# Five small edits in a two-block transformer kernel: dispatch order, slot weights, value width, two queue orders

## The chip, the cores and the metric

The kernel runs on one core of a Trainium2 chip and is written in Bass with the Tile framework, which sets the semaphores between the engines from the tiles that instructions read and write. The metric is the device time of one execution in microseconds, given as the median of several executions.

## What is computed

All data is fp32: 256 tokens of 1024 features. A first block mixes the tokens by a pooling branch and by a differential attention of 8 heads, merges the two by gates, and ends with a feed-forward layer of 4096 hidden features. A second block has latent attention and neighbourhood attention over the tokens and a context of 256 more, and then a mixture of experts in 4 groups of 4. Each token takes one group and two experts of it. Cut to what the change touches:

```python
# first block
h = rmsnorm(x, g_mix)
z = h @ w_in                       # pool 512 | queries 1024 | keys 1024 | values 1024 columns
v = z[..., 2560:3584]
# second block: hx, hc are the normalised, modulated tokens and context
proj = hx @ w_in_2                 # q_lat 384 | na_q 512 | kv_lat 256 | kr 32 | na_k 512 | na_v 512
nk_c, nv_c = (hc @ w_in_2)[..., 672:1184], (hc @ w_in_2)[..., 1184:]
# mixture of experts: g_sel is each token's group, combine its two expert weights
hid = silu(t @ w_gate[e]) * (t @ w_up[e])
y = sum over e of (hid * combine[:, e]) @ w_down[e]
```

The inputs are drawn from a fixed seed, so each group's number of tokens is the same in every execution.

## The kernel before, in words

**Products in three parts.** Up to the experts every fp32 factor is cut into an upper part, rounded to the type `fp32r`, and a lower part, the rest. A product is then three matmuls: upper by upper, upper by lower, lower by upper (`mm3`, or written out in `dense_steps`). Weights come by DMA as blocks of 128 x 2048 into one of four raw buffers. All these loads are issued by SP in the order of the program. `split` (lines 188 to 194) cuts a piece of 1024 columns: ScalarE copies the upper part (line 192) and VectorE subtracts it to get the lower part (line 193). A block takes two such calls.

**Order of the work.** A planner, `J`, runs several generators beside one another. Each yields the TensorE time of what it has just issued (`MM` stands for the three matmuls of 256 columns) or a waiting time or a condition; the planner takes the next step from the lane with the best rank that is ready by its own clock. The result is a fixed order of instructions for each engine; at run time each engine works through its own in order. `order(later, earlier)` sets such an order by hand.

**First block.** The lane `feed` (lines 710 to 729) issues two blocks of the pooling input (`upool`), then for each of four pairs of heads the query block, the key block and the value block `v_block(p)` (lines 540 to 554), then eight gate blocks. Beside it run `stats` (lines 490 and on) and two lanes of attention heads. `stats` computes the squares of x, their means by TensorE (`ms`), the sum `mse` on VectorE (line 498), and from it the root and its reciprocal `rcol`. `v_block` multiplies 8 pieces of the tokens by 256 columns of weights, for each half of the tokens, into one bank of PSUM; the halves share the bank. `scaled_split` then writes the upper part on ScalarE and the lower on VectorE. `mmbank` gives the banks for query, key, value and gate blocks in turn.

**Second block.** `na_values` (lines 954 to 971) does the same for the values of the neighbourhood attention, first for the context, then for the tokens, in two blocks of 256 columns each. `na_pair` (lines 981 to 1004) makes queries and keys for two heads. The lower part of the queries, `ql`, is written twice, to two ranges of partitions, by two VectorE steps per head (lines 999 and 1001).

**Routing and experts.** The tokens of a group are gathered into slots by a product with a one-hot matrix (`gather`, name `xg`, line 1658). A group with more than 64 tokens is *wide* and has 128 slots. Six programs for the experts are in the kernel, called ways here: ways 0 to 3 where one group is wide, the group of that number; way 4 where all are; way 5 in two passes. The number is in memory (`way`); each engine loads it into a register (line 1907) and finds its program by nested comparisons (`ways_from`, lines 1909 to 1923). Its `tc.If` at line 1918 is a COMPARE_BRANCH instruction on each engine's sequencer. In each program 16 turns follow, one for each expert, in the order of `TURNS`: groups 0 and 1 by turns, then groups 2 and 3. A turn has 32 gate and up products (`gate_up`, name `gu`, lines 1765 to 1776), the activation `hidden`, a transposition and 16 or more products with `w_down` (name `y`). `product` makes TensorE keep the written order of all of them. `slot_weights` (lines 1737 to 1748) takes the routing weights of each slot by 16 small products (`sv`), which `gate_up(0, slot_weights)` places between its 16th and 17th product. `hidden` multiplies by these weights. The expert weights are 96 blocks of 1 MB, loaded into a ring of 17 buffers, each load being issued by SP as soon as its buffer has been used.

Of the kernel before, what the change touches and what calls it, by code (L numbers as in the profile page):

```python
# [15 lines left out]
OP = mybir.AluOpType  # L16
# [58 lines left out]
IDLE = (13, 7)  # L75

KEPT = 5

HALF = 64

# [41 lines left out]
def tile_two_blocks(ctx, tc, a):  # L122
# [65 lines left out]
    def split(src, n):  # L188
        t = whl.tile([128, 2048], F32R, name="whl", tag="w")
        hi, lo = t[:, 0:n], t[:, 1024:1024 + n]  # L190
        with tc.high_priority(offset=AHEAD_SPLIT):
            nc.scalar.copy(hi, src)  # L192
            nc.vector.tensor_sub(lo, src, hi)  # L193
        return hi, lo

    def split_fine(w):

# [292 lines left out]
    def stats():  # L490

        with low_priority(SQP):
            acc = squares(xT)
        use_table("natural_log_exp_and_others")
        yield 0, LAT_ST
        ms = bank(7, "ms")
        mean_mm(ms, acc)
        nc.vector.tensor_scalar(mse, ms[:, :2], EPS, None, op0=OP.add)
        nc.vector.tensor_scalar(epsq, mse, EPS, None, op0=OP.mult)
        rstd(rcol, mse, 2)  # L500
        yield 0.43, 2.0
        rb_ps = bank(7, "rb_ps")
        rows_of_cols(rb_ps, rcol)
        nc.vector.tensor_copy(rb, rb_ps[:, :T])
        small_inputs()
        yield 0.86, 0.5, when("u")
        for b in range(2):
            nc.vector.tensor_mul(upad[:, 2 * b:2 * b + 2, 16:], ups[b].rearrange("p (m t) -> p m t", m=2),
                                 rb.unsqueeze(1).to_broadcast([128, 2, T]))
        wg = big(11, [128, 2, 512], F32R, "wg")  # L510
        wgh, wgl = wg[:, 0], wg[:, 1]
        copy_split(wgh, wgl, load(a["w_grp"], (128, 512)))
        for g in range(4):
            yield 0, LAT_POOL
            pool_group(g, wgh, wgl)
            yield 0.35
# [22 lines left out]

    def v_block(b):  # L540

        w = split_block(load(a["w_in"][10 + b]))
        ps = mmbank("v")
        for tb in range(2):
            for k in range(8):
                hi, lo = w(k, 256)
                mm3(ps[:, tb * 256:(tb + 1) * 256],
                    (xh[:, k, tb * 128:(tb + 1) * 128], xl[:, k, tb * 128:(tb + 1) * 128]), (hi, lo),
                    k == 0, k == 7)
                yield MM  # L550
        for tb in range(2):
            scaled_split(vh[:, tb, b * 256:(b + 1) * 256], vl[:, tb, b * 256:(b + 1) * 256],
                         ps[:, tb * 256:(tb + 1) * 256], rcol[:, tb:tb + 1])
        done.add(("v", b))

    def gate_block(g):
        half, j = divmod(g, 4)
# [152 lines left out]
    def feed():  # L710
        for b in range(2):
            ups.append(bank(3 + b, "upool"))
            if b == 0:
                yield from dense_steps(ups[b], split_fine(first), xs, groups=[range(i, i + 2) for i in range(0, 8, 2)])
            else:
                yield from dense_steps(ups[b], split_block(load(a["w_in"][b])), xs)
        done.add("u")
        for p in range(4):
            if p >= 2:
                yield 0, 0, lambda: pair[p - 2]["heads"] == 2  # L720
            yield from qk_block(p, 0)
            yield from qk_block(p, 1)
            yield from v_block(p)
            for i in MODQ[p]:
                mod_block(i, MODS.get(i))
        for n, g in enumerate((0, 4, 1, 5, 2, 6, 3, 7)):
            yield from gate_block(g)
            for i in MODG[n]:
                mod_block(i, MODS.get(i))
# [222 lines left out]
    nav = [value_tile(7), value_tile(8)]  # L952

    def na_values():
        wv = [split_block(load(a["w_in2"][4 + b])) for b in range(2)]
        yield
        for n in range(2):
            if n == 1:
                yield "context"
                yield 0, 3.0, when("hx")  # L960
            for b in range(2):
                ps = mmbank("nav")
                for tb in range(2):
                    for k in range(8):
                        mm3(ps[:, tb * 256:(tb + 1) * 256],
                            (srcs[n][0][:, k, tb * 128:(tb + 1) * 128], srcs[n][1][:, k, tb * 128:(tb + 1) * 128]),
                            wv[b](k, 256), k == 0, k == 7)
                        yield MM
                for tb in range(2):
                  with tc.high_priority(offset=NAVP):  # L970
                    value_split(nav[n], tb, slice(4 * b, 4 * b + 4), ps[:, tb * 256:(tb + 1) * 256])

    def proj(ps, w, c0, n, kt=8, width=256, x=None, koff=0):

# [6 lines left out]
    def na_pair(p):  # L981
# [15 lines left out]
        for j in range(2):  # L997
            nc.scalar.activation(qh[j][rows[j]], psq[rows[j]], AF.Copy, scale=0.125)
            nc.vector.scalar_tensor_tensor(ql[j][rows[j]], psq[rows[j]], 0.125, qh[j][rows[j]], op0=OP.mult, op1=OP.subtract)
            nc.scalar.activation(qh[j][rows[1 - j]], psq[rows[j]], AF.Copy, scale=0.125)  # L1000
            nc.vector.scalar_tensor_tensor(ql[j][rows[1 - j]], psq[rows[j]], 0.125, qh[j][rows[j]], op0=OP.mult,
                                           op1=OP.subtract)
        J.add(0, ready(("na", p), 1.2))
        pair["na", p] = qh, ql, keys, nb

# [667 lines left out]
    def experts(part, wide):  # L1673
# [193 lines left out]
                with tc.high_priority(offset=CHAIN):  # L1867
                    sums[g] = finish(g)

        gate_up(0, slot_weights)  # L1870
        if TURNS[0][0] in wide or TURNS[1][0] in wide:
            rows_of_slots()
        for n in range(16):
# [7 lines left out]
            else:  # L1881
                if n > 0:
                    list(down(n - 1))
                early = n == 0 and not {TURNS[0][0], TURNS[1][0]} & set(wide)
                if early:
                    gate_up(1)
                turn(n)
# [21 lines left out]
    def ways_from(lo, hi):  # L1909

        if hi - lo == 1:
            table["load"], table["uses"] = None, []
            experts(0, (lo,) if lo < 4 else tuple(range(4)))
            if lo == 5:
                experts(1, tuple(range(4)))
            return
        mid = (lo + hi) // 2 if hi <= 4 else max(lo + 1, 4)
        with tc.If(n_way < mid) as cmp:
            ways_from(lo, mid)
        with cmp.Else():  # L1920
            ways_from(mid, hi)
# [26 lines left out]
def layout(i):  # L1948
# [9 lines left out]
    o["cols"] = np.ascontiguousarray(np.concatenate([cols_of(p) for p in parts], axis=1))  # L1958
    o["lambda_qk"] = i["lambda_qk"].reshape(1, 256)
    o["w_in"] = blocks(i["w_in"][0], 256)  # L1960
    o["w_gate"] = blocks(i["w_gate"][0], 256)
    o["w_grp"] = np.ascontiguousarray(i["w_pool_grp"][0].transpose(1, 0, 2).reshape(128, 512))
    o["w_bp"] = blocks(i["w_branch_pool"][0], 512)
# [20 lines left out]
    o["b_mod"] = np.ascontiguousarray(i["b_mod_2"][0].reshape(6, D))  # L1984
    w = i["w_in_2"][0]
    q_lat, na_q, kv_lat, kr, na_k, na_v = np.split(w, np.cumsum([384, 512, 256, 32, 512]), axis=1)
    sw = np.concatenate([kr[:, 16:], kr[:, :16]], axis=1)
    pairs = [p for m in range(4) for p in (na_k[:, m * 128:(m + 1) * 128], na_q[:, m * 128:(m + 1) * 128])]
    o["w_in2"] = blocks(np.concatenate(pairs + [na_v, kv_lat, kr, sw, kr, sw, q_lat[:, 256:], q_lat[:, :256]],
# [50 lines left out]
        rt[:, 16 + 2 * tb] = np.arange(128) + tb * 128  # L2040
        rt[:, 17 + 2 * tb] = 1.0
    rt[:, 20] = np.arange(128) + FAR
    rt[:, 21:25] = np.arange(4) + 8.0
    o["rt"] = rt
    o["iota"] = np.ascontiguousarray(np.broadcast_to(np.arange(1, 513, dtype=f)[None], (128, 512)))
    o["before"] = (np.arange(128)[:, None] < np.arange(128)[None, :]).astype(f)
# [6 lines left out]
```

## Time and profile before

| | |
|---|---|
| median of three executions | 875.27 us (875.26 to 877.39) |
| the profiled execution | 877.89 us |
| its span in the trace | 876.1 us |
| TensorE busy | 850.8 us, 97% |
| VectorE busy | 559.7 us, 64% |
| ScalarE busy | 425.9 us, 49% |
| DMA, mean over the span | 256 GB/s |

Times of rows are microseconds from the start of the span. PE is TensorE's matmul part and PEld its weight load, which overlaps with matmuls; DVE is VectorE, ACT ScalarE, SP the engine that issues the loads. A q behind an engine's name (PEldq, SPq) is its sequencer: register, branch and DMA-issuing instructions. A matmul's duration in a row runs from its start to its modelled end and overlaps with the next one's; the pace of a row of matmuls is read from the starts. "[1.25 <-DVE whl L193]" behind a row says that the engine was idle for 1.25 us ahead of it, and which instruction it had waited for. [...]

### The profile page before, as it was taken

To read this page: it belongs to the slowest core of one execution; us is meant where nothing else is said; L and a number is where in the kernel's file an instruction comes from. 1 tells how busy PE (TensorE), PEld (TensorE's weight loads), DVE (VectorE), ACT (ScalarE), POOL (GpSimd) and SP (SyncE) were. 2 spreads that over 40 slices of the span, in tenths; PEclk is the share of its full clock that TensorE was granted. 3 is DMA by queue.
4 is the path that set the end of the run, shared out by engine and by line. 5 is a ranking of instruction groups with operands and counts; after the bars stand their busy time and mean duration, and the time that the engine had idled before them with its cause. 6 is when DMAs were issued, how large, how long until landed. Compare 5 with 4: busy or idle time off the path is not lost. (4 is left out here: it accounts for less than half of the span.)

```text
span 876.1 us, 14580 instructions
## 1 busy us (share of the span) xinstructions
PE 850.8 (97%) x5827; PEld 691.9 (79%) x5827; DVE 559.7 (64%) x1137; ACT 425.9 (49%) x800; POOL 15.4 (2%) x28
## 2 busy tenths in 40 slices
PE   8999999999999999999999999999989999999995
PEld 7998999999999999999999988889943333334331
DVE  6898778799988768777855899997741111111104
ACT  6487787744564555546754687797520000000002
POOL 1000000000000000000000000000001000001001
PEclk9999999999999999999999999999899999999998
DMA  7762555577887665768524225546879999999970
GB/s 278 276 246 97 183 177 198 205 266 272 316 300 266 232 251 203 282 206 303 190 78 144 97 79 186 191 144 237 335 263 416 426 427 427 426 426 427 425 315 33
DMA packets 34781, 224.51 MB, mean 256 GB/s; under 512 B 4479, under 2 KB 6143, under 8 KB 8458
## 3 DMA queue, kind: packets, MB, share of 16 engines
q1 hardware_dynamic: 31256, 216.18, 65.3%
q10 hardware_dynamic: 2674, 5.16, 1.6%
q0 software_dynamic: 768, 2.10, 0.6%
q8 instruction: 49, 0.80, 0.4%
q14 instruction: 34, 0.28, 0.1%
HBM read 220.53 MB, written 3.41 MB: 256 GB/s over the span
## 5 line engine op out<-in xcount | busy, mean ns | idle before, releaser
L192 ACT CAST whl<-w 128x1024 fp32r<-128x1024 f32 x155 | 161.9, 1048 | 121.2 <-PE up L251 46.3
L193 DVE TENSOR_TENSOR whl<-w,whl 128x1024 fp32r<-128x1024 f32 x155 | 188.0, 1220 | 42.5 <-ACT whl L192 41.9
L1754 PE MATMUL gu<-w,XG 128*64 128x512 f32 (+1 forms) x512 | 142.7, 603 | 2.5 <-issue 2.5
L1754 PEld LDWEIGHTS gu<-w,XG 128*64 128x64 f32 (+1 forms) x512 | 51.2, 151 | 81.9 <-issue 81.2
L155 ACT ACTIVATE sg<-gu 64x512 f32<-64x512 f32 (+1 forms) x16 | 9.4, 590 | 192.0 <-PE gu L1754 192.0
L896 PE MATMUL dn<-hh,whl 128*128 128x256 f32 x512 | 93.2, 280 | 0.0
L1786 DVE SCALAR_TENSOR_TENSOR h<-sg,small,gu 64x512 f32<-64x512 f32 (+1 forms) x16 | 12.0, 751 | 121.0 <-ACT sg L155 67.5
L406 DVE SCALAR_TENSOR_TENSOR macc<-w,cs,macc 128x512 f32<-128x512 f32 x104 | 74.4, 745 | 9.8 <-DMA w<-w_mod 9.8
L896 PEld LDWEIGHTS dn<-hh,whl 128*128 128x128 f32 x512 | 79.8, 189 | 0.0
L249 PE MATMUL up<-fh,whl 128*128 128x256 f32 x256 | 73.2, 286 | 0.0
L250 PE MATMUL up<-fl,whl 128*128 128x256 f32 x256 | 72.4, 283 | 0.0
L251 PE MATMUL up<-fh,whl 128*128 128x256 f32 x256 | 72.4, 283 | 0.0
L1754 PE MATMUL y<-w,th 128*64 128x512 f32 (+1 forms) x256 | 72.2, 596 | 0.0
L896 PE MATMUL dn<-hl,whl 128*128 128x256 f32 x256 | 72.1, 282 | 0.0
L1754 PEld LDWEIGHTS y<-w,th 128*64 128x64 f32 (+1 forms) x256 | 25.0, 150 | 42.5 <-issue 41.3
L250 PEld LDWEIGHTS up<-fl,whl 128*128 128x128 f32 x256 | 49.1, 192 | 0.1
L251 PEld LDWEIGHTS up<-fh,whl 128*128 128x128 f32 x256 | 49.1, 192 | 0.0
L249 PEld LDWEIGHTS up<-fh,whl 128*128 128x128 f32 x256 | 49.0, 192 | 0.0
L896 PEld LDWEIGHTS dn<-hl,whl 128*128 128x128 f32 x256 | 48.1, 188 | 0.0
L249 PE MATMUL gate<-xh,whl 128*128 128x256 f32 x128 | 36.9, 288 | 0.0
L1797 DVE COPY th<-tpe 128x256 f32<-128x256 f32 (+1 forms) x16 | 7.8, 490 | 45.1 <-PE tpe L1754 45.1
L250 PE MATMUL gate<-xl,whl 128*128 128x256 f32 x128 | 36.3, 283 | 0.0
(515 smaller groups left out, 2123.3 us busy)
## 6 DMA issues: line engine op xcount, KB each, us to landing
w<-e_gate SPq DMA_DIRECT2D x32, 1024.0 KB, 19.6
w<-e_up SPq DMA_DIRECT2D x32, 1024.0 KB, 18.5
w<-e_down SPq DMA_DIRECT2D x32, 1024.0 KB, 19.5
w<-w_mod SPq DMA_DIRECT2D x24, 1024.0 KB, 5.2
w<-w_in SPq DMA_DIRECT2D x22, 1024.0 KB, 5.3
w<-w_up SPq DMA_DIRECT2D x16, 1024.0 KB, 7.0
w<-w_down SPq DMA_DIRECT2D x16, 1024.0 KB, 4.8
w<-w_gate SPq DMA_DIRECT2D x8, 1024.0 KB, 6.2
```

Of the source, the lines that this page charges most:

```text
L155: i = nc.scalar.activation(*args, **kw).ins
L192: nc.scalar.copy(hi, src)
L193: nc.vector.tensor_sub(lo, src, hi)
L249: matmul(o, hi[:, c], x[0], start=n == 0, stop=False, skip_group_check=True)
L250: matmul(o, hi[:, c], x[1], start=False, stop=False, skip_group_check=True)
L251: matmul(o, lo[:, c], x[0], start=False, stop=last, skip_group_check=True)
L406: nc.vector.scalar_tensor_tensor(m, src, c, m, op0=OP.mult, op1=OP.add)
L896: matmul(o, u, v, start=start and n == 0, stop=stop and n == 2, skip_group_check=True)
L1754: i = matmul(*args, **kw).ins
L1786: nc.vector.scalar_tensor_tensor(hs[n][0:m], sg[r], sv[r, g, 4 * g + i:4 * g + i + 1], gu[n][1], op0=OP.mult, op1=OP.mult)
L1797: nc.vector.tensor_copy(hs[n][:, 0:4 * m], tp[:, 0:4 * m])
```

## The change

1. The ways are asked for one after another, in the order of the new table `WAYS = (2, 3, 0, 1)`, and the number in memory counts by this table.
2. Where neither of the first two turns is of a wide group, the slot weights stand behind all 32 products of `gate_up(0)`.
3. `v_block` works on 512 columns of weights: it runs for the first and third pair alone, makes two sums, one for each half of the tokens, in two banks, and takes its weights as two loads (`w_v`), each half of the 1024 rows. The steps run over the halves of the rows first, then over those of the tokens.
4. `na_values` works on 512 columns in the same way, one bank for each half of the tokens, weights `w_nav`.
5. `mse` is ordered behind the first two lower parts that `split` writes.
6. The second `ql` of each head is copied by ScalarE from the first, in place of a second VectorE step.

```diff
+WAYS = (2, 3, 0, 1)
...
             nc.scalar.copy(hi, src)
-            nc.vector.tensor_sub(lo, src, hi)
+            lows.append(nc.vector.tensor_sub(lo, src, hi).ins)
...
-        nc.vector.tensor_scalar(mse, ms[:, :2], EPS, None, op0=OP.add)
+        summed = nc.vector.tensor_scalar(mse, ms[:, :2], EPS, None, op0=OP.add).ins
+        for i in lows[:2]:
+            order(summed, i)
...
     def v_block(b):
-        w = split_block(load(a["w_in"][10 + b]))
-        ps = mmbank("v")
+        pv = [mmbank("v") for _ in range(2)]
+        for kh in range(2):
+            w = split_block(load(a["w_v"][b][:, kh * 2048:(kh + 1) * 2048]))
+            for tb in range(2):
+                for k2 in range(4):
+                    k = 4 * kh + k2
+                    t = slice(tb * 128, (tb + 1) * 128)
+                    mm3(pv[tb], (xh[:, k, t], xl[:, k, t]), w(k2, 512), k == 0, k == 7)
+                    yield 2 * MM
         for tb in range(2):
-            for k in range(8):
-                hi, lo = w(k, 256)
-                mm3(ps[:, tb * 256:(tb + 1) * 256],
-                    (xh[:, k, tb * 128:(tb + 1) * 128], xl[:, k, tb * 128:(tb + 1) * 128]), (hi, lo),
-                    k == 0, k == 7)
-                yield MM
-        for tb in range(2):
-            scaled_split(vh[:, tb, b * 256:(b + 1) * 256], vl[:, tb, b * 256:(b + 1) * 256],
-                         ps[:, tb * 256:(tb + 1) * 256], rcol[:, tb:tb + 1])
-        done.add(("v", b))
+            scaled_split(vh[:, tb, b * 512:(b + 1) * 512], vl[:, tb, b * 512:(b + 1) * 512], pv[tb], rcol[:, tb:tb + 1])
+        done.update((("v", 2 * b), ("v", 2 * b + 1)))
...
-            yield from v_block(p)
+            if p % 2 == 0:
+                yield from v_block(p // 2)
...
-        wv = [split_block(load(a["w_in2"][4 + b])) for b in range(2)]
+        wv = [split_block(load(a["w_nav"][0][:, kh * 2048:(kh + 1) * 2048])) for kh in range(2)]
...
-            for b in range(2):
+            for tb in range(2):
                 ps = mmbank("nav")
-                for tb in range(2):
-                    for k in range(8):
-                        mm3(ps[:, tb * 256:(tb + 1) * 256],
-                            (srcs[n][0][:, k, tb * 128:(tb + 1) * 128], srcs[n][1][:, k, tb * 128:(tb + 1) * 128]),
-                            wv[b](k, 256), k == 0, k == 7)
-                        yield MM
-                for tb in range(2):
-                  with tc.high_priority(offset=NAVP):
-                    value_split(nav[n], tb, slice(4 * b, 4 * b + 4), ps[:, tb * 256:(tb + 1) * 256])
+                t = slice(tb * 128, (tb + 1) * 128)
+                for k in range(8):
+                    mm3(ps, (srcs[n][0][:, k, t], srcs[n][1][:, k, t]), wv[k // 4](k % 4, 512), k == 0, k == 7)
+                    yield 2 * MM
+                with tc.high_priority(offset=NAVP):
+                    value_split(nav[n], tb, slice(0, 8), ps)
...
-            nc.vector.scalar_tensor_tensor(ql[j][rows[1 - j]], psq[rows[j]], 0.125, qh[j][rows[j]], op0=OP.mult,
-                                           op1=OP.subtract)
+            nc.scalar.copy(ql[j][rows[1 - j]], ql[j][rows[j]])
...
-        gate_up(0, slot_weights)
+        narrow_first = not {TURNS[0][0], TURNS[1][0]} & set(wide)
+        gate_up(0, None if narrow_first else slot_weights)
+        if narrow_first:
+            slot_weights()
...
-            experts(0, (lo,) if lo < 4 else tuple(range(4)))
+            experts(0, (WAYS[lo],) if lo < 4 else tuple(range(4)))
...
-        mid = (lo + hi) // 2 if hi <= 4 else max(lo + 1, 4)
+        mid = lo + 1
...
-    rt[:, 21:25] = np.arange(4) + 8.0
+    rt[:, 21:25] = np.argsort(WAYS) + 8.0
```

## Rows read from the trace of the kernel before

**Rows 1.** The page: busy us, share of the span and instructions of each engine.

```profile
PE 850.8 (97%) x5827; PEld 691.9 (79%) x5827; DVE 559.7 (64%) x1137; ACT 425.9 (49%) x800; POOL 15.4 (2%) x28
```

**Rows 2.** Attention stage: busy PE, PEld, DVE, ACT, POOL (count); PEclk, DMA share, GB/s.

```profile
465.00:620.00 155.00, 150.38 (x1105) 138.79 (x1104) 125.83 (x291) 111.86 (x225) 0.00 (x0) 1.00 0.47 168
```

**Rows 3.** TensorE's waits: one line, us in total, times, longest us.

```profile
PE gu L1754 <- issue: 2.5, 1, 2.5
```

**Rows 4.** Timeline from 14 us: start, duration, engine, line, operation, [idle before].

```profile
14.39 2.00 ACT L192 CAST whl<-w 128x1024 fp32r<-128x1024 f32 x2 [0.21 <-DMA w<-w_in]
...
17.20 0.16 DVE L498 TENSOR_SCALAR mse<-ms 128x2 f32<-128x2 f32 x1 [1.58 <-PE ms L369]
17.22 0.28 PE L250 MATMUL upool<-xl,whl 128*128 128x256 f32 x1
...
17.47 2.36 DVE L193 TENSOR_TENSOR whl<-w,whl 128x1024 fp32r<-128x1024 f32 x2
...
18.75 0.38 PE L251 MATMUL upool<-xh,whl 128*128 128x256 f32 x1 [1.25 <-DVE whl L193]
```

**Rows 5.** TensorE's sequencer from 638 us: durations in ns, first and last start.

```profile
L1918 PEldq COMPARE_BRANCH  x1: 92/92/92, 638.1 to 638.1; - x1
...
L1918 PEldq COMPARE_BRANCH  x1: 3865/3865/3865, 638.3 to 638.3; - x1
```

**Rows 6.** First expert products: timeline, a later step of the chain, two stretches' clock.

```profile
642.44 5.35 PE L1754 MATMUL gu<-w,XG 128*64 128x512 f32 x16 [2.45 <-issue]
647.72 1.96 PE L1754 MATMUL sv<-small,S 128*128 128x16 f32 x16
...
665.48 7.02 PE gu L1754 x32
...
642.80:646.20 3.40, 3.40 (x10) 1.20 (x8) 0.65 (x4) 0.00 (x0) 0.00 (x0) 0.50 0.73 289
626.00:630.00 4.00, 4.00 (x21) 4.00 (x20) 2.56 (x14) 3.20 (x8) 0.00 (x0) 0.50 0.76 239
```

**Rows 7.** Timeline of VectorE: last routing step, copies of the slot weights.

```profile
643.36 0.19 DVE L1606 TENSOR_TENSOR small<-ohr,small 128x32 f32<-128x32 f32 x1
...
649.72 0.25 DVE L1748 COPY small<-sv 64x16 f32<-64x16 f32 x2 [0.73 <-PE sv L1754]
650.00 0.18 DVE L1746 COPY small<-sv 128x16 f32<-128x16 f32 x1
```

**Rows 8.** Timeline of TensorE: first and last of rows of value products.

```profile
61.79 0.28 PE L222 MATMUL v<-whl,xh 128*128 128x256 f32 x1
...
63.47 0.28 PE L224 MATMUL v<-whl,xl 128*128 128x256 f32 x1
...
546.01 0.39 PE L222 MATMUL vm<-whl,kvn 128*128 128x512 f32 x1
...
547.16 0.39 PE L224 MATMUL vm<-whl,kvn 128*128 128x512 f32 x1
```

**Rows 9.** Timeline: the third pair's value block, last product and last lower part.

```profile
100.36 0.29 PE L224 MATMUL v<-whl,xl 128*128 128x256 f32 x1
...
107.22 0.48 DVE L321 SCALAR_TENSOR_TENSOR vl<-v,rcol,vh 128x256 fp32r<-128x256 f32 x1
```

**Rows 10.** Loads of expert weights: issues (KB, us to landing), and an eighth-turn product.

```profile
647.79 0.33 SPq L1356 DMA_DIRECT2D w<-e_up  x1
...
710.00 0.33 SPq L1356 DMA_DIRECT2D w<-e_up  x1
...
w<-e_up SPq DMA_DIRECT2D x4, 1024.0 KB, 19.6
...
730.45 1.98 PE L1754 MATMUL gu<-w,XG 128*128 128x512 f32 x4
```

**Rows 11.** The copied lower part of the queries (ns), and a wait in that stage.

```profile
L1001 DVE SCALAR_TENSOR_TENSOR napair<-naq,napair x8: 419/422/428, 474.8 to 536.9; 64x256 fp32r<-64x256 f32 x8
...
PE s L1016 <- DVE mx L1026: 1.1, 2, 0.7
```

More of the change, by code (lines that the diff above doesn't have):

```diff
@@ L192, in split @@
             nc.scalar.copy(hi, src)
-            nc.vector.tensor_sub(lo, src, hi)
+            lows.append(nc.vector.tensor_sub(lo, src, hi).ins)
         return hi, lo
+    lows = []
     def split_fine(w):
@@ L1883, in experts @@
                     list(down(n - 1))
-                early = n == 0 and not {TURNS[0][0], TURNS[1][0]} & set(wide)
+                early = n == 0 and narrow_first
                 if early:
@@ L1960, in layout @@
     o["w_in"] = blocks(i["w_in"][0], 256)
+    o["w_v"] = blocks(i["w_in"][0][:, 2560:3584], 512)
     o["w_gate"] = blocks(i["w_gate"][0], 256)
@@ L1986, in layout @@
     q_lat, na_q, kv_lat, kr, na_k, na_v = np.split(w, np.cumsum([384, 512, 256, 32, 512]), axis=1)
+    o["w_nav"] = blocks(na_v, 512)
     sw = np.concatenate([kr[:, 16:], kr[:, :16]], axis=1)
```

## The prediction

> **What bounds the kernel now.** I read the busy times first, then TensorE's waits, then the places of the waits in the timeline, and at the branch the sequencer's own instructions. TensorE has work for 850.8 us of a span of 876.1 [rows 1]; even in the attention stage, where VectorE is busy 125.8 of 155 us, TensorE is busy 150.4 [rows 2]. So almost everywhere the time is the sum of TensorE's instructions, and an edit gains in only two ways: it makes those instructions shorter, or it removes one of the few places where TensorE stands still. Two such places belong to this change: 2.5 us ahead of the first expert products, with no releaser but "issue" [rows 3], and 1.25 us in the first stage, behind a VectorE subtraction [rows 4].
>
> **First lower parts ahead of the sums.** ScalarE writes the two upper parts of the second weight block from 14.39 to 16.39. VectorE could subtract from about 15.4 on, but the sum of squares `mse` stands ahead in its queue and waits for TensorE until 17.20; the two subtractions run from 17.47, 2.36 us for both. TensorE issues the product of 17.22 and the next only at 18.75 [rows 4]. At the pace of 0.12 us a product [rows 8] that one would have come at 17.34, so the stall costs 1.41 us. With the new order the first subtraction runs from about 15.4 to 16.6 and the second, whose input is there at 16.39, to about 17.8. What is late then is `mse`: 17.8 instead of 17.20. Behind it in VectorE's queue stand the other steps of the root; on ScalarE the logarithm, and behind that the copies of the third block, wait 0.6 us longer. But before, the last steps of the root stood behind those same subtractions, until 19.83, so they do not end later. I take -1.4; the bounds are 0 (another part is late at once) and -1.5.
>
> **Ways asked for in another order.** Only one group's slots are copied at full height (the one copy at line 1746, third of four groups by its place): group 2 is wide, the way number is 2 [rows 7]. The old tree asks "below 4" (yes), "below 2" (no), "below 3" (yes). TensorE's sequencer passes the first compare, at 638.1, in 0.092 us; the second, the one answered no, holds it for 3.865 us, from 638.3 to 642.1 [rows 5]. Only then come the gate products: 642.44, after 2.45 us of idle time [rows 6], so the gathers ended at 639.99. In the new table group 2 is way 0, and the first question is "below 1", answered yes. A yes falls through, at 0.09 us; no compare answered no is left on this path. The sequencer is then through at about 638.2, 1.8 us before the last gather product ends, and nothing else is shown as holding the gate products. I take -2.45; a floor of 0 holds if the fetch comes all the same.
>
> The gap has a second price. [...] The first 16 gate products took 5.35 us; later, at the full clock, 32 of them take 7.02 us, so 16 take 3.51 [rows 6]. The loss is 1.84 us. Without the gap TensorE goes from dense gathers straight into dense gate products, and I expect no fall: -1.84, bounds 0 and -1.84. Compares for the other ways cost nothing here: this input never reaches them.
>
> **Slot weights behind the first gate products.** The same 16 small products, 1.96 us [rows 6], only change place. They need the routing weights, whose last VectorE step ends at 643.55 [rows 7]. With the gate products starting at 640.0, half of them end at 643.5: in the old place the slot weights would now just meet that step. Behind all 32 products, at 647, they do not wait. Who waits for them is the first hidden product on VectorE, and that is read by TensorE only behind the second turn's 7.02 us of gate products. I take 0; without that cover it would be up to 2.0.
>
> **Do the expert weights keep up?** The ring of 17 buffers makes this the place where the gain could be handed on. The first load that waits for a consumed buffer is issued at 647.79, when the first half of the gate products is done; later loads land 19.6 us after issue, in a queue that is always full, so the one issued at 710.00 is there at 729.6, and its turn's products begin at 730.45 [rows 10]. The margin is about 1 us, so TensorE may not run ahead of its loads. It does not: the release at 647.79 moves by the same 4.3 us as the products, and the two releases behind it lose the slot weights in front of them as well. I take 0; bounds -0 and +3.3 (4.3 less the margin, if no load moves).
>
> **Values by 512 columns.** The two places have 192 products of 256 columns each; they become 96 of 512. Fourteen intervals of 256-column products take 61.79 to 63.47, 0.120 us each; five of 512 columns take 546.01 to 547.16, 0.230 us [rows 8]. Two narrow ones cost 0.240, so a pair saves 0.010: 96 x 0.010 = 0.96 us in each place. In the first stage TensorE is dense, and I take -0.9. In the second, half the products wait for the second stream's normalised tokens, a VectorE and ScalarE chain that the change does not shorten, so I take half, -0.4. Bounds for both together: 0 and -1.9. The same bytes are loaded by as many loads, in the same order of blocks, and the evacuations are half as many at less than double length; VectorE and ScalarE have idle time beside them.
>
> [...]
>
> **Lower part of the queries copied by ScalarE.** Eight VectorE steps of 0.42 us leave, eight ScalarE copies of the same 64x256 arrive. In that stage TensorE's longest waits for VectorE are 1.1 us for the running maximum [rows 11], so at most about that is gained; the copy now waits for the VectorE step before it, and attention scores wait for the copy, which could cost the 0.42 of one step for each of four pairs, 1.7. I take 0, bounds -1.1 and +1.7.
>
> **The sum.** -2.45 - 1.84 - 1.4 - 0.9 - 0.4 = -7.0 us. The profiled execution took 877.89 us, 1.8 more than its span of 876.1, and stands 2.6 above the median of 875.27; the terms are taken from it and subtracted from the median: 868.3 us.
>
> **Rivals.**
> *Only the gap goes, the clock falls all the same.* The routing ahead is made of small products, and the trace has one more stretch of low clock there, 0.50 from 626 to 630 us, with TensorE busy all 4 us of it [rows 6]; the clock could fall once more. Then 1.84 is not gained: 870.1. Against it: the gathers right before the branch run at full clock.
> *The loads do not follow.* TensorE then waits up to 3.3 us in the eighth turn: 871.6. For it: the 1 us of margin; against it: the release moves with the products.
> *The change doesn't do what it says at the branch.* If the first body is also fetched late, 4.3 us stay: 872.6. Against it: the compare of 0.092 us that fell through [rows 5].
> *The wide product keeps the pace per column.* Then the 1.3 is lost: 869.6. The two intervals above speak against it.
> *The value block holds both product banks* (the slower side). Its two sums take banks 0 and 1 at once, and the next query block's product takes bank 0 at once. In the third pair's block the last product was issued at 100.36 and the last lower part began at 107.22, 0.48 us long [rows 9]: 7 us until the bank was free, which nobody waited for since the next group had the other bank. If TensorE waits that long in both value blocks, 14 us are added to 868.3: 882.3. It makes the kernel slower once the two waits together exceed 7.0. Against it: the first sum now ends 12 wide products (2.8 us) before the second, the third bank serves the key block, and attention products of other heads can fill in.
> *VectorE's relief frees the attention stage*: -1.1, 867.2.
>
> **How the numbers follow.** Chances: the forecast 0.55, clock 0.10, loads 0.08, branch 0.08, pace 0.05, banks 0.07, relief 0.07. The range takes in the forecast, relief, pace, clock, loads and branch cases, and below the forecast the untaken half of the second value place and ScalarE's copy: 866.0 to 873.0; the bank case is left out, with part of the branch case. A measurement of this kernel can tell about 0.3%, 2.6 us, from no change: faster is below 872.6, slower above 877.9. All of forecast, clock, loads, pace and relief are faster (0.85), of the branch case and of half-priced bank waits most are the same (0.09), the rest slower (0.06).
>
> **What would show it.** Right: TensorE's idle time ahead of the first gate product below 0.3 us, one compare on its sequencer; the granted clock at 1.00 through the first turn; the second `upool` block without its 1.25 us; 512-column value products 0.23 us apart; no expert product waiting for a load. Wrong: a compare of over 3 us that stays; a query block waiting for ScalarE's or VectorE's evacuation of the values; a wait for `e_up` in the eighth turn; a wait for the copied lower part at the scores.

## The result and the profile after

The changed kernel took 866.7 us (866.6 to 868.0) where the kernel before took 876.3 beside it: a ratio of 0.989, 95% interval 0.986 to 0.993. The forecast was 868.3. One kernel's executions differ by several microseconds here, and the mean granted clock goes with them (0.987 in an execution of the kernel before of 881.19 us, 0.996 in one of 871.75): it stands at 0.50 for a few microseconds at places that change from one execution to the next, in one trace of the changed kernel from 623.6 to 627.0 us, in its second one from 625.0 to 628.2. Over all executions beside the experiments the median of the kernel before is 875.7 (86 executions; one more, of 1044.6 us at a mean granted clock of 0.75, is set aside) and that of the changed one 867.0 (10).

The page's first part of the changed kernel (busy us, share, instructions), to be held against [rows 1]:

```profile
PE 844.0 (98%) x5635; PEld 675.6 (78%) x5635; DVE 556.0 (64%) x1121; ACT 426.6 (49%) x800; POOL 15.3 (2%) x28
```

192 products are gone and 6.8 us of TensorE's busy time. The span fell by 11.4, so 4.6 us of idle time went as well, net.

Its list of TensorE's waits (us in total, times, longest), against [rows 3]:

```profile
PE both L1757 <- ACT sqz L1834: 2.8, 1, 2.8
PE pos L1519 <- DVE ohr L1501: 1.8, 1, 1.8
PE warm L294 <- DVE ones_r L283: 1.4, 1, 1.4
PE pv L227 <- ACT sbias L690: 1.4, 2, 1.1
...
PE upool L256 <- DVE whl L195: 0.2, 1, 0.2
```

The wait for "issue" is not there any more, the one of 1.25 us in the first stage [rows 4] is 0.2, and no expert product waits for a load. New is 1.8 us in the routing, ahead of `pos`. It comes back below.

The dispatch, on TensorE's sequencer (ns) and in its timeline, against [rows 5] and [rows 6], with the clock of the first turn's products (stretch; us, busy PE, PEld, DVE, ACT, POOL, PEclk, DMA share, GB/s; PEclk is TensorE's granted clock, 1.00 at full speed):

```profile
L1924 PEldq COMPARE_BRANCH  x1: 88/88/88, 631.4 to 631.4; - x1
```

```profile
633.19 7.09 PE L1757 MATMUL gu<-w,XG 128*64 128x512 f32 x32
640.21 1.96 PE L1757 MATMUL sv<-small,S 128*128 128x16 f32 x16
```

```profile
633.20:640.20 7.00, 7.00 (x33) 2.20 (x32) 4.72 (x19) 1.30 (x2) 0.00 (x0) 1.00 0.97 338
```

One question instead of three, 0.09 us. The gate products follow the gathers without idle time, and all 32 run at the full clock in 7.09 us, where 16 had taken 5.35.

To see where the rest came from I cut both spans at the starts of the same products. TensorE works in nearly the same order in all these kernels, so the stages add up, and a single edit shows in its own stage. Times are us, from the first or last product of a name in one timeline each:

| from ... to | before | changed | with one edit alone |
|---|---|---|---|
| start ... last `upool` | 24.25 | 21.84 | lower parts first: 21.28 |
| ... last `gate` | 156.85 | 154.34 | values by 512: 154.17 |
| ... first `nav` | 243.14 | 243.12 | |
| ... first `nak` | 38.67 | 37.47 | neighbourhood values by 512: 37.45 |
| ... first `xg` | 169.37 | 167.62 | `ql` by ScalarE: 168.45 |
| ... first `gu` | 10.16 | 8.81 | ways: 7.70 |
| ... first `tpe` | 17.62 | 15.92 | ways: 16.03 |
| ... last `y` | 204.28 | 204.27 | |

A stage that no edit touches and in which the clock does not fall agrees within 0.02 us (third and last row). In such a stage differences of some tenths can be read, far below what the times of whole executions allow. The rows that end at the first `xg` and the first `gu` are not such stages: in ten of the fourteen traces of this case the clock stood at half somewhere in them, for 6.6 us of the first of the two in the kernel before, 5.5 with `ql` alone and 0.8 in the changed kernel. A difference in them is not the price of an edit by itself.

### The profile page after: what moved, and what is told of

Read it like the earlier page. It is cut to its first block, busy times and chain, and to the rows that moved or that the text cites. A ratio compares the mean times of both kernels' runs of the same rounds, so it can differ in the third digit from the quotient of the medians.

```text
span 864.7 us, 14168 instructions
## 1 busy us (share of the span) xinstructions
PE 844.0 (98%) x5635; PEld 675.6 (78%) x5635; DVE 556.0 (64%) x1121; ACT 426.6 (49%) x800; POOL 15.3 (2%) x28
## 4 chain that ended last, share of the span: by engine, by line
PE 75%; ACT 11%; DVE 9%; DMA 2%; issue 2%; SPq 0%; POOL 0%; ACTq 0%; POOLq 0%; DVEq 0%
PE gu L1757 16%; PE dn L903 10%; PE y L1757 8%; PE up L254 3%; PE up L255 3%; PE up L256 3%; ACT whl L194 3%; DVE whl L195 3%; ACT sbias L157 2%; PE s L1019 1%; DMA w<-w_mod 1%; ACT p L157 1%; DMA w<-w_in 1%; PE xg L1661 1%; PE wo L255 1%
## 6 DMA issues: line engine op xcount, KB each, us to landing
w<-e_gate SPq DMA_DIRECT2D x32, 1024.0 KB, 19.6
w<-e_up SPq DMA_DIRECT2D x32, 1024.0 KB, 18.5
w<-e_down SPq DMA_DIRECT2D x32, 1024.0 KB, 19.6
```

## The experiments

**The ways alone.** The kernel before with the table and the linear questions:

```diff
+WAYS = (2, 3, 0, 1)
-            experts(0, (lo,) if lo < 4 else tuple(range(4)))
+            experts(0, (WAYS[lo],) if lo < 4 else tuple(range(4)))
-        mid = (lo + hi) // 2 if hi <= 4 else max(lo + 1, 4)
+        mid = lo + 1
-    rt[:, 21:25] = np.arange(4) + 8.0
+    rt[:, 21:25] = np.argsort(WAYS) + 8.0
```

> The kernel before with the new order of the ways alone (the table, one question after another); slot weights, values and queue orders stay as they were. Theory of the prediction: the idle time of 2.45 us ahead of the first gate products goes, with it the clock's fall behind it (1.84 us): 4.3 us less, 871.0 against 875.3, and the trace shows one compare of about 0.1 us on TensorE's sequencer. Rival, the clock falls all the same: 2.45 less, 872.8, with granted clock 0.50 in the first turn. Rival, the first program's code is fetched late too: no gain, a compare or a gap of over 2 us stays. Second rival for the slot weights: in their old place they now meet the routing's last VectorE step and give back up to 1 us.

Measured: 871.4 (median of 12), ratio 0.995 (0.992 to 0.997). Its timeline of TensorE and the clock of the first products:

```profile
640.18 3.65 PE L1756 MATMUL gu<-w,XG 128*64 128x512 f32 x16
643.87 1.96 PE L1756 MATMUL sv<-small,S 128*128 128x16 f32 x16
```

```profile
640.20:643.90 3.70, 3.67 (x18) 1.07 (x17) 3.04 (x15) 1.28 (x2) 0.00 (x0) 1.00 1.03 365
```

From the first `xg` to the first `gu` it is 2.46 us faster than the kernel before, from there to the first `tpe` another 1.59: together 4.05 of the 4.29 expected. The first figure can be read so because the clock ahead was alike in these two traces, at half until 632.9 and 632.6. Over all traces the idle time at this place was 2.45 to 3.22 us in five with a "no" of 3.8 to 3.9 us, and nothing in the six without a "no". The clock does not fall, so that rival is out. In all eight traces of kernels with a "no" on the path, the clock stood at 0.50 during the first gate products: it fell 0.4 to 1.1 us behind the first of them in five, and already within the gap in the three whose gap was 5.8 to 9.5 us. None of the six without a "no" has a fall between the branch and the end of the turns.

**Three questions, three times yes.** The same table, but with the old halving of the interval:

```diff
-        mid = lo + 1
+        mid = (lo + hi) // 2 if hi <= 4 else max(lo + 1, 4)
```

> The kernel before with the new table of the ways but the old nested halving: three questions on the way to the wide group's program, all three answered yes. Theory, only a no costs: three compares of about 0.1 us on TensorE's sequencer, no idle time ahead of the first gate product, as in the run with one question (871.4). Rival, the number of questions counts: idle time of 2 us and more ahead of the gate products, about 875. The first stage is that of the kernel before: where the granted clock fell again at 17 to 21 us in four of the six earlier traces with that stage, a fall here or a late rise past 13.9 us is expected if the wait of 1.25 us has to do with it, none if it is chance.

```profile
L1920 PEldq COMPARE_BRANCH  x3: 65/65/95, 638.2 to 638.5; - x3
```

Three compares, none over 0.1 us, no idle time for "issue", 872.2 (median of 8): what counts is the answer. In this trace the clock did fall, at 637.4, but behind a wait of the gathers for ScalarE (1.95 us) and not behind the branch. So from the first `xg` to the first `tpe` it is only 0.35 us ahead of the kernel before, and the gain shows in the sequencer and in the times, not in that stage. What was expected of the first stage did not come: the wait of 1.25 us was there, the clock reached full speed at 12.8 us and did not fall again.

**Two times no.** The changed kernel with the ways in the order 0, 1, 2, 3:

```diff
-WAYS = (2, 3, 0, 1)
+WAYS = (0, 1, 2, 3)
```

> The changed kernel with the ways one after another in the order 0, 1, 2, 3, so that the wide group of these inputs is the third asked for: two questions answered no instead of none. Theory, a no costs its code: two compares of about 3.9 us each stand on TensorE's sequencer, 1.8 us of it covered by the gathers, so about 6 us of idle time ahead of the first gate product, and with the clock's fall of 1.8 us some 8 us more than the changed kernel: 874.5. Rival, only the first jump is dear (the code behind it is fetched on): about 2.5 us idle, 870.9. Rival, the number of questions matters and not the answer: 0.1 us for each, no difference.

Measured: 878.8 (median of 12, 877.2 to 881.8), 11.8 above the changed kernel (11.4 in the traces) and 2.5 above the kernel before beside it (876.3). Sequencer, timeline and clock:

```profile
L1924 PEldq COMPARE_BRANCH  x1: 3811/3811/3811, 631.2 to 631.2; - x1
L1924 PEldq COMPARE_BRANCH  x1: 7177/7177/7177, 635.0 to 635.0; - x1
L1924 PEldq COMPARE_BRANCH  x1: 70/70/70, 642.3 to 642.3; - x1
```

```profile
642.52 9.12 PE L1757 MATMUL gu<-w,XG 128*64 128x512 f32 x32 [9.50 <-issue]
```

```profile
636.50:646.60 10.10, 4.08 (x10) 1.38 (x12) 1.76 (x5) 0.00 (x0) 0.00 (x0) 0.50 0.22 84
```

Each no has its price, 3.81 and 7.18 us; the second is nearly twice the first. My 8 us more were too few by 3.4, which is what the second compare took above 3.8. A no of 6.2 and one of 6.8 us also stand in one trace each of two kernels below that keep the old tree; in the other five traces with the old tree it is 3.84 to 3.90. Beside each no stands a DMA packet of 16 KB that the trace lists as `instruction`; those of this size are all on queue q8. The DMA view of the kernel before, from 638 to 642 us, has one:

```profile
q8 instruction: 1, 0.02, 1.8%
```

It ran from 639.55 to 640.69, and the compare answered no ended at 642.14. Each of the nine compares answered no in the fourteen traces ended 1.41 to 1.55 us behind such a packet. In the six traces without a no, none lies within 1.6 us of a compare. The packet began 1.1 to 1.5 us after the start of the compare in the six of 3.81 to 3.90 us, and 3.1 to 4.3 us after it in the three long ones; in the one of 7.2 us it also took 2.6 us, where it took 0.9 to 1.4 in the others. That a no waits for this packet, and is long where the packet comes late, is my reading of these times; it is not shown, since no run moves that packet by itself, and why it came late in the three is not settled. The other engines pay as well, beside the critical path: in the kernel before, the compare behind the no starts 2.45 us after it on SP, 2.89 on VectorE and 0.4 on ScalarE and POOL, against 0.03 to 0.04 behind a yes.

**First lower parts ahead of the sum, alone.**

```diff
-            nc.vector.tensor_sub(lo, src, hi)
+            lows.append(nc.vector.tensor_sub(lo, src, hi).ins)
...
+        for i in lows[:2]:
+            order(summed, i)
```

> The kernel before with the first two lower parts ordered ahead of the sum, alone. Theory of the prediction: the wait of 1.25 us in the second upool block goes, 1.4 us less, 873.9. What the two traces say by now: up to the last upool product the changed kernel is 2.41 us ahead, 1.65 of it before the stall, where its granted clock rose at 9.2 us instead of 14.7. Rival: the clock's early rise is the execution's, not the change's; then this run gains 0.8 us with the clock rising at the same time as in the kernel before beside it, and its own trace may show the rise at either time.

Measured: 874.7 (median of 12), ratio 0.999 (0.996 to 1.002), too little for times to tell. The trace tells it: the wait is gone.

```profile
15.62 0.28 PE L253 MATMUL upool<-xl,whl 128*128 128x256 f32 x1
15.78 0.39 PE L254 MATMUL upool<-xh,whl 128*128 128x256 f32 x1
```

0.16 us lie between the two products that stood 1.53 apart in [rows 4]: 1.37 us less, in the stage's end 2.97. The other 1.6 stand ahead of the wait: the first of the two products starts at 15.62 here and at 17.22 in the kernel before. Ahead of it the clock's first record at full speed begins at 12.5 us here and at 14.7 in the kernel before (9.2 to 14.0 in the other traces); in the kernel before a product starts every 0.21 us up to that record and every 0.12 behind it. That the 1.6 belong to this execution I read from all fourteen traces. In the eight with the old order the last `upool` product starts at 23.1 to 24.4 (mean 23.7), in the six with the new one at 21.3 to 22.3 (mean 21.75). In four of the eight the clock stood at half again for 3.4 us, from 16.7 to 18.5 us on, soon behind the wait, as in the trace of the ways alone:

```profile
18.60:21.80 3.20, 3.20 (x17) 3.20 (x16) 3.17 (x8) 0.47 (x1) 0.00 (x0) 0.50 0.81 284
```

In none of the six does it. The two old-order traces that have neither this fall nor a rise of the clock past 13.9 us end at 23.1: 1.35 above the mean of the six, which fits the 1.37 between the two products and is the price of the wait itself. So the edit is worth 1.35. The means of all traces are 0.6 further apart, but that this is the falls' is not shown: the four traces with a fall end at 23.2 to 24.4 (mean 23.8), the four others with the old order at 23.1 to 24.3 (mean 23.6). The falls came in the four old-order traces whose clock had risen first, at 9.9 to 11.7 us. In four of the six with the new order it had risen by 11.8 as well and did not fall, so the wait does seem to have to do with the fall.

**Values by 512 columns, alone**, with `v_block` as in the change:

```diff
-            yield from v_block(p)
+            if p % 2 == 0:
+                yield from v_block(p // 2)
```

> The kernel before with the first block's values by 512 columns, alone. Theory of the prediction: only the pace, 96 pairs by 0.010 us, 0.9 us less, 874.4. The two traces show 2.5 us gained between the last upool product and the last gate product. Rival: that is the change's too, by fewer switches between value products and other work and by shorter waits there; then this run gains about 2.5 us, 872.8. Second rival: the waits of that stretch went for reasons of order that only the whole change has; then 0.9 or less.

Measured: 873.5 (median of 12), ratio 0.997 (0.995 to 1.000), and 154.17 instead of 156.85 in its stage: 2.7 us, not 0.9. (The stage takes 156.8 to 157.4 in six traces with the old values and 153.9 to 154.4 in six with the new ones; a seventh with the old ones, in which the clock fell at 157.3 us, takes 158.7.) The pace is as the prediction had it; in the changed kernel the first and last of eight products in a row:

```profile
87.07 0.39 PE L228 MATMUL v<-whl,xh 128*128 128x512 f32 x1
...
88.68 0.39 PE L229 MATMUL v<-whl,xl 128*128 128x512 f32 x1
```

Seven intervals of 0.230, as in [rows 8]. So 1.7 us come from elsewhere. TensorE stands idle for 3.7 us of the stage in the kernel before and for 2.4 here, so 1.3 of them are shorter waits.

**The new arrangement with narrow products.** The same blocks, banks, loads and evacuations, each product as two of 256 columns:

```diff
-                    mm3(pv[tb], (xh[:, k, t], xl[:, k, t]), w(k2, 512), k == 0, k == 7)
+                    hi, lo = w(k2, 512)
+                    for n in range(2):
+                        c = slice(n * 256, n * 256 + 256)
+                        matmul(pv[tb][:, c], xh[:, k, t], hi[:, c], ...)
+                        matmul(pv[tb][:, c], xh[:, k, t], lo[:, c], ...)
+                        matmul(pv[tb][:, c], xl[:, k, t], hi[:, c], ...)
```

> The first block's values in the new arrangement (first and third pair only, two banks, two loads of 512 columns, the sums half as many and twice as long), but each product of 512 columns made as two of 256. The run with 512 columns gained 2.6 us between the last upool product and the last gate product. Theory of the prediction, the pace: at 0.010 us a pair, 96 pairs, this run loses 0.96 us of that, so 1.6 us stay as the arrangement's. Rival, all is the product's width: then no gain stays, or less than 0.3. Rival, all is the arrangement: the 2.6 us stay.

Measured: 877.5 (median of 10), ratio 1.001 (0.999 to 1.004). Its stage takes 158.01: 1.16 more than before, 3.84 more than with wide products. TensorE's longest waits in it, up to 125 us:

```profile
PE st L591 <- ACT sq L581: 1.0, 2, 0.6
PE v L554 <- DVE whl L193: 0.9, 1, 0.9
PE tp L678 <- DVE am L672: 0.5, 1, 0.5
```

The arrangement by itself loses; the width wins it back and 2.7 more. So of the expectations the one that puts the whole gain down to the products' width came nearest, and the 1.6 us of the prediction's theory did not stay. Of the 3.84 the pace is 1 us, and 2.3 are waits: over the whole stage TensorE is idle for 4.7 us, against 2.4 with wide products. The remaining 0.6 have no row. Why the planned order meets VectorE and ScalarE better with wide products is not taken apart further: width and order change together, since the scheduler places the rest anew around them.

**Neighbourhood values by 512 columns, alone**, with `na_values` as in the change:

```diff
-        wv = [split_block(load(a["w_in2"][4 + b])) for b in range(2)]
+        wv = [split_block(load(a["w_nav"][0][:, kh * 2048:(kh + 1) * 2048])) for kh in range(2)]
```

> The kernel before with the neighbourhood values by 512 columns, alone. Theory of the prediction: half of the 0.96 us of pace, 0.4 us less, 874.9, with the rest lost in waits for the second stream's tokens. Rival: the whole pace and more, since TensorE is dense there as well: the two traces show 1.27 us gained from the first value product to the next stage, so 874.0.

Measured: 873.6 (median of 12), ratio 0.997 (0.995 to 0.999); the stage takes 37.45 instead of 38.67, 1.22 us less. The whole pace is gained and 0.26 on top. The time of the execution fell by more than the stage can explain (2.0 by medians); with the spread of the executions I hold to the stage.

**Slot weights alone**, in the old tree:

```diff
-        gate_up(0, slot_weights)
+        gate_up(0, None if narrow_first else slot_weights)
+        if narrow_first:
+            slot_weights()
```

> The kernel before with the slot weights behind the first gate products, alone, the ways asked for as before. Theory of the prediction: nothing, 875.3: the same 16 products, 1.96 us, in another place. Rival: with the gap and the low clock still there, 16 more gate products run at the low clock ahead of the slot weights, or the clock rises earlier because of denser work: up to 1 us either way.

Measured: 875.3 (median of 12), ratio 0.999 (0.997 to 1.000): nothing. Its profiled execution, the slowest of the twelve at 880.0, has the no of 6.8 us:

```profile
L1921 PEldq COMPARE_BRANCH  x1: 6805/6805/6805, 636.5 to 636.5; - x1
```

With the ways changed, the place of the slot weights can be read from the stage of the first turn: 16.03 with them in the middle, 15.92 behind, 0.1 us.

**The lower part of the queries.** First the copy alone in the kernel before:

```diff
-            nc.vector.scalar_tensor_tensor(ql[j][rows[1 - j]], psq[rows[j]], 0.125, qh[j][rows[j]], op0=OP.mult,
-                                           op1=OP.subtract)
+            nc.scalar.copy(ql[j][rows[1 - j]], ql[j][rows[j]])
```

> The kernel before with the second lower part of the queries copied by ScalarE, alone. Theory of the prediction: nothing, 875.3 (bounds 1.1 less to 1.7 more). The two traces show 1.7 us gained between the first neighbourhood keys and the last attention product, where this is the only edit in the code. Rival: the relief of VectorE is worth that much, 873.6. Second rival: the 1.7 us are a new order of the lanes that the planner chose because the values finished earlier; then this run shows no gain.

Measured: 876.7 (median of 12), ratio 1.001 (0.999 to 1.003). Then the changed kernel with the VectorE step back:

> The changed kernel with the second lower part of the queries written by VectorE again. Theory of the prediction: the copy by ScalarE is worth nothing, so 866.7 as the changed kernel. Rival: the relief is worth 1.1 to 1.7 us, so 867.8 to 868.4 and longer waits for VectorE in the attention stage of the second block.

Measured: 865.9 (median of 6). As this was on the good side, both were run again beside each other:

> The changed kernel once more, beside the next one: 866.7 to 867.0. With the first lower parts ahead of the sum, no fall of the granted clock at 17 to 21 us is expected, as in none of the four traces of kernels with that order.

> The changed kernel with the second lower part of the queries on VectorE again, for more executions: the traces differ by 0.4 us between the neighbourhood keys and the first gate products in its favour, the run with that edit alone shows 0.4 the other way. Theory of the prediction, the copy is worth nothing: the same as the changed kernel within 0.5 us. Rival, the copy costs up to 1.2 us: 865.6.

Measured: 867.3 with the copy and 865.6 without (medians of 6 each; ratios to the kernel before 0.989, 0.986 to 0.993, and 0.988, 0.9845 to 0.9915). With the earlier executions, the means are 867.2 (10) and 866.0 (12), 1.1 apart with a standard error of 0.5. The copy costs about 1 us, and the traces show where. With the copy, TensorE's timeline at the end of the stage:

```profile
613.83 0.97 PE L1458 MATMUL lg<-route,x2T 128*128 128x20 f32 x8
614.65 0.36 PE L1381 MATMUL wo<-oT,whl 128*128 128x256 f32 x1
...
616.90 0.33 PE L1449 MATMUL xps<-ident,x2T 128*128 128x128 f32 x1 [0.58 <-DVE x2T L1444]
...
622.61 0.27 PE L1519 MATMUL pos<-ohr,before 128*128 128x8 f32 x1 [1.83 <-DVE ohr L1501]
```

Without it:

```profile
614.34 0.28 PE L1384 MATMUL wo<-oT,whl 128*128 128x256 f32 x1
614.46 0.38 PE L1450 MATMUL xps<-ident,x2T 128*128 128x128 f32 x2
...
621.32 0.27 PE L1520 MATMUL pos<-ohr,before 128*128 128x8 f32 x1
```

The copy did not delay anything at its own place; there the last scores (`s`) come 5.2 us earlier with it (591.8 against 597.0). It changed TensorE's order: routing logits `lg` are issued ahead of the last twelve residual products `wo`, so the routing's norm, which needs the last residual, starts later (last `wo` 616.0 against 614.3, 0.5 of it from ahead of the stage), and TensorE waits 1.83 us for its result. In all four traces with the copy the clock falls to half within the routing (in this one from 625), in the two without it and with all else changed it does not (in those of kernels with few edits it does in some):

```profile
625.00:628.20 3.20, 3.20 (x9) 2.53 (x8) 2.12 (x8) 1.54 (x3) 1.70 (x1) 0.50 0.62 225
```

Where the clock does not fall between the first `nak` and the first `xg`, that stage takes 167.59 us with the copy (one trace) and 166.8 to 166.9 in five of the six traces without it (167.3 in the sixth): 0.7 to 0.8 of the 1.1 are there. The 168.45 of the copy alone against 169.37 before, in the table of stages, stand under 5.5 and 6.6 us of low clock and say nothing of it.

The kernel without the copy is thus the better one, 865.7 by the median of its twelve executions. It was found by these runs, and nothing else in it was tuned.

## Why the prediction was right, point by point

| step | predicted | measured |
|---|---|---|
| ways, idle time | -2.45 | -2.46 |
| ways, clock | -1.84 | -1.59 |
| first lower parts | -1.4 | -1.35 (means of all traces: -1.9) |
| values by 512 | -0.9 | -2.7 |
| neighbourhood values by 512 | -0.4 | -1.2 |
| `ql` by ScalarE | 0 (-1.1 to +1.7) | +1.1 (means of executions) |
| slot weights | 0 | -0.1 |

The measured terms add up to -8.3, or -8.9 with the means for the start; by the medians of all executions it was 8.7 less, against 7.0 predicted. The 866.7 lie 0.7 above the lower end of the range.

- The dispatch was right in cause and size. One reading carried it: the compare answered yes took 0.092 us and the one answered no 3.865 [rows 5]. That the price hangs on the no, and not on the number of questions, two runs confirm: three compares answered yes took 0.065 to 0.095 us each, two answered no 3.81 and 7.18. That every further no costs again, up to twice as much, was not in the prediction. The fetch of which it speaks was my estimate and is not shown by any run; what the traces show is an `instruction` packet that ended 1.41 to 1.55 us before the end of each no.
- The low clock behind the gap went with the gap, as predicted: 0.50 from 642.8 to 646.2 us before [rows 6], 1.00 through the first gate products in the changed kernel and with the ways alone. Its loss went with it. The 0.25 missing of its 1.84 lies in how the prediction set its two figures: 5.35 runs to the modelled end of the last product, and 3.51 is half of a row of 32. From the first gate product to the first of the slot weights it was 5.28 us before [rows 6] and 3.69 with the ways alone, a difference of 1.59.
- The start was right in its 1.4. That low clock follows the wait there in four of the eight old-order traces was not seen, since the one trace of before was an execution without that fall.
- The value term is the one that was mis-sized: I priced the products by their pace and took every other wait in the stage as staying. The pace held, at 0.230 us for 512 columns against 0.240 for two of 256 [rows 8], and the waits shrank, by 1.3 of the 1.7 us that the term was short; they are shorter only with wide products, as the run with narrow ones shows. In the neighbourhood values I halved the pace's gain for a wait on the second stream's tokens that the trace of before does not show as TensorE's wait; the full gain came.
- The copy by ScalarE lay inside its bounds, for another reason than the bound on the slower side stood for: not the scores waited for the copy, but TensorE's order changed 100 us later. Its +1.1 took back part of what the values gave beyond their term, so that the sum was nearer than its parts. That is luck: with the copy at the 0 that it was priced at, as the kernel without it shows, the median is 865.7, below the 866.0 where the range ends.
- Of the rivals, those on the clock, the branch and the pace fell by the granted 1.00 of the first turn, the compare of 0.09 us and the 0.230 us of a wide product. The bank rival fell: TensorE waits for no value evacuation in either value block. The loads followed: the load that answers to the one of 710.00 [rows 10] was issued at 699.36, and its turn's products (the ninth turn's, by the rows of 32; the prediction calls it the eighth) began at 719.50 without idle time.

```profile
699.36 0.33 SPq L1359 DMA_DIRECT2D w<-e_up  x1
...
719.50 2.84 PE L1757 MATMUL gu<-w,XG 128*128 128x512 f32 x6
```

By the 19.6 us to landing of [rows 10] that load was there at 719.0, 0.5 us ahead of its products, where the same count gives 0.85 before. So load and products moved together, and the margin stayed under 1 us.

## What to carry to other kernels

Where engines choose among programs at run time, put the likeliest one on the path on which each compare is answered yes (0.065 to 0.095 us here, against 3.8 to 7.2 for a no), and look for a long compare on the sequencer behind an idle time whose releaser is only "issue"; here the low clock behind such a gap of 2.45 us cost another 1.59. On an engine that is busy 97% of the span, cut the traces at the same products and compare stage by stage: in a stage where the clock does not fall, a few tenths of a microsecond can be read so, where whole executions differ by several. Look up first where the clock fell in each trace. An edit that is free at its own place can still cost where the scheduler answers it with another order, so run such an edit alone before it is kept.

## What the runs showed of the hardware

- At the dispatch a compare answered yes took 0.065 to 0.095 us on TensorE's sequencer in all runs; one answered no took 3.8 to 3.9 us in most, and 6.2, 6.8 and 7.2 us in three. Each no ended 1.41 to 1.55 us behind a DMA packet of 16 KB that the trace lists as `instruction`.
- The granted clock fell to 0.50 behind each gap at the dispatch of 2.5 to 3.2 us, while TensorE went on with dense work, and within the gaps of 5.8 to 9.5 us: the low stretch at the gap of 9.5 us covers 636.5 to 646.6, shown above, of which 6 us were the gap itself.
- With the same code, the 86 executions of the kernel before took 871.7 to 883.9 us. The mean granted clock goes with it: 0.996 in one of 871.75, 0.987 in one of 881.19.
